# Holding the last products of two matrix products in source order, bank by bank

## The chip, the cores and the metric

The kernel runs on one core of one Trainium2 chip. The metric is the device time of one execution in microseconds (us). TensorE (PE) multiplies, VectorE (DVE) and ScalarE (ACT) do the elementwise work, GpSimd (POOL) a little of it, and SyncE (SP) issues most of the transfers. Each engine works through its own instruction list in order, and engines wait for each other by semaphores.

## The reference

One decoder layer over 256 tokens of width 1024, in float32, with three token mixers side by side:

```python
merged = (gates[:, :, 0] * (o_a @ w_br_a[i])
          + gates[:, :, 1] * (o_b @ w_br_b[i])
          + gates[:, :, 2] * (o_c @ w_br_c[i]))
x = layer_norm(ALPHA * x + merged @ w_out[i], ln1_g[i], ln1_b[i])
h = jnp.square(jax.nn.relu(x @ w_up[i])) @ w_down[i]
ple = jax.nn.sigmoid(x @ w_ple_gate[i]) * (p[i] @ w_ple[i])
x = layer_norm(ALPHA * x + h + ple, ln2_g[i], ln2_b[i])
```

The change touches the product `merged @ w_out` (the output projection) with the first layer norm behind it, and the product with `w_down` (the down projection) with the second layer norm behind it.

## The kernel before, in words

**Arithmetic.** Every float32 operand is split into a high part and a low part (`hi`, `lo`), and a product of two operands is three matmuls: high by high, high by low, low by high. `prod` (L131 to L135) issues these three. A weight tile of 128 x 1024 is loaded by SP into `raw`, ACT copies it into the high part (L75), and DVE subtracts to get the low part (L79). Five such tiles are in flight (`raw` and `part` have five buffers).

**Order.** The program is written in one sequence; a scheduler with a timing model of its own then chooses the order on every engine, by what it expects to be ready first. Two means bind it: `tc.high_priority`, and `tc.keep_in_program_order(m)`, which holds an instruction behind the ones so marked before it on its engine. Before the change only the attention logits (L271) are marked.

**The output projection** (`Wide`, L525 to L553). The 256 tokens are two halves `b` of 128 rows, the 1024 columns two halves `c` of 512; each (b, c) has a PSUM bank: `b0_2962` and `b1_2963` for the rows of b = 0, `b3_2964` and `b2_2965` for b = 1. `step` runs the first four of eight weight tiles over all banks. `finish` (L545) is written for the last four: bank by bank, and behind each bank `ln1` is called (`done`). A bank takes 12 matmuls there, 4 tiles by 3.

**The first layer norm** (`ln1`, L620 to L638). For each bank DVE forms `Y = ALPHA * x + acc` (L622) and its statistics (L605). After both banks of a half b it combines them (L610), adds epsilon (L611), POOL takes the power -1/2 (L612), and DVE normalises in four passes of 512 columns: two that subtract the mean (L617), two that scale (L619). Then PE transposes the rows (L632, eight 128 x 128 blocks for a half), and ACT and DVE split the transposes into high and low (L634, L635) as `x1`. `x1` is the stationary operand of the gate projection `pg` (banks `b2_3337`, `b4_3338`, `b0_3339`, `b1_3340`), which starts with two weight tiles of b = 0 (12 matmuls), and the moving operand of the up projection that follows.

**Filler.** Between the two stand 24 matmuls of `p @ w_ple` (6 for each of the banks `mm_3305`, `mm_3313`, `mm_3321`, `mm_3329`), which wait for none of this. ACT writes their result into `PL` (L651), where `ln1` has read x before.

**The down projection.** Most of its weight tiles are done earlier; the last six (`LAST = 6`, four in `part` tiles, two in the place of `x1`) go bank by bank: `b0_4526` and `b4_4513` for b = 0, then `b1_4533` (512 columns), `b3_5014` and `b2_5015` (256 columns each) for b = 1, 18 matmuls a bank. Behind each bank `ln2` (L815) adds `PL` and takes the statistics; after the last bank of a half it normalises and SP stores the rows.

Of the kernel before, what the change touches and what calls it, by code (L numbers as in the profile page):

```python
# [40 lines left out]
LAST = 6  # L41
# [52 lines left out]
def hybrid_layer(ctx: ExitStack, tc: tile.TileContext, x0, xn, pT, wqk, wva, wvb, wg, wbc, wba,  # L94
                 wout, wup, wdq, wdn, wpg, wple, lnrow, rel, onehot, pick, out):
    nc = tc.nc
    pe, act, dve, pool = nc.tensor, nc.scalar, nc.vector, nc.gpsimd
# [30 lines left out]
    for _ in range(13):  # L128
        pe.transpose(t[:, 0:128], ident, ident)  # L129

    def prod(ps, a, b, first, last):  # L131

        pe.matmul(ps, lhsT=a[0], rhs=b[0], start=first, stop=False)  # L133
        pe.matmul(ps, lhsT=a[0], rhs=b[1], start=False, stop=False)  # L134
        pe.matmul(ps, lhsT=a[1], rhs=b[0], start=False, stop=last)  # L135

    def gemm(ps, units, xs, k=0):

        for u in units:
            hi, lo = W.get(u)  # L140
            for o in range(0, hi.shape[1], 128):
                prod(ps, (hi[:, o:o + 128], lo[:, o:o + 128]), xs[k], k == 0, k == len(xs) - 1)
                k += 1
# [61 lines left out]
    def mmbank(shape):  # L205
        t = mm.tile([128, 512], F32, name="mm", tag="mm")
        return t[:, 0:256] if shape == 256 else t

    last = [None]
# [9 lines left out]
    def k_pair(a, b=None):  # L219


        k = (kp if b is None else k1).tile([128, 2, S], F32R, name="k", tag="k")
        for d, ps in ((slice(0, 128), a),) if b is None else ((slice(0, 64), a),
                                                             (slice(64, 128), b)):
            act.copy(k[d, 0], ps)
            dve.tensor_tensor(k[d, 1], ps, k[d, 0].bitcast(F32), op=ALU.subtract)
        return k
# [3 lines left out]
    def fill(what):  # L231


        for w in what:
            if w == "g":
                ps = mmbank(256)
                gemm(ps, u_g[n_g[0]], xs)
                act.activation(G[:, n_g[0]], ps, AF.Tanh, scale=0.5)
                n_g[0] += 1
                continue  # L240
            f = n_c[0]
            n_c[0] += 1
            hi, lo = W.get(u_bc[f][0])
            ps = mmbank(512).rearrange("p (i s) -> p i s", i=2)
            for i, (k0, k1) in enumerate(((3, 5), (5, 8))):
                for k in range(k0, k1):
                    c = slice((k - 3) * 128, (k - 2) * 128)
                    prod(ps[:, i], (hi[:, c], lo[:, c]), (op[:, k, 0], op[:, k, 1]), k == k0,
                         k == k1 - 1)
            g = G[:, 3 * f + 1:3 * f + 3]  # L250
            dve.scalar_tensor_tensor(g, g, 1.0, ps, op0=ALU.add, op1=ALU.mult)  # L251
            dve.tensor_tensor(g[:, 0], g[:, 0], g[:, 1], op=ALU.add)

    def feat(f):
        ps = mmbank(256)
        gemm(ps, u_q[f], xs)
        if f > 4:
            next(side, None)
        return ps
# [21 lines left out]
    def values(units, n, h0, heads, withiw):  # L281
        pss = [mmbank(512) for _ in range(2)]
        for i in range(4):
            hi, lo = W.get(units[i])
            for j in range(2):
                k = 2 * i + j
                c = slice(j * n, (j + 1) * n)
                for b in range(2):
                    t = slice(b * 128, (b + 1) * 128)
                    prod(pss[b][:, :n], (xh[:, k, t], xl[:, k, t]), (hi[:, c], lo[:, c]),  # L290
                         k == 0, k == KT - 1)
        v_out(pss, n, h0, heads, withiw)
# [95 lines left out]
    with ExitStack() as begin:  # L388
# [4 lines left out]
        with tc.high_priority(offset=1000):  # L393
# [4 lines left out]
            for k in range(KT):  # L398
                act.copy(xh[:, k], g0[:, k, 0:S])
                for a, b in cut[k]:  # L400
                    a = max(a, S)
# [3 lines left out]
        first = [next(ps_s if f < 3 else ps_t)[:, 0:S] for f in range(FIRST)]  # L405
        for k in range(KT):
            for i, (w, x) in enumerate(((sh, xh), (sh, xl), (sl, xh))):
                for f in range(FIRST):
                    pe.matmul(first[f], lhsT=w[:, k, 128 * f:128 * f + 128], rhs=x[:, k],  # L409
                              start=k == i == 0, stop=k == KT - 1 and i == 2)  # L410
# [3 lines left out]
    ps = feat(4)  # L414
# [36 lines left out]
    for j in range(2):  # L451
        ps = feat(5 + 4 * j)
        k = k_pair(ps)
# [17 lines left out]
    for j in range(3):  # L471
        ps = feat(13 + 2 * j)
        k = k_pair(ps)
# [50 lines left out]
    class Wide:  # L524
# [3 lines left out]
            self.units, self.stat, self.cut, self.ws = units, stat, cut, {}  # L528
            self.acc = [[next(ps_a)[:, 0:hi - lo] for lo, hi in c] for c in cut]

        def go(self, k, b, c):
            h, l = self.stat(k, b)
            cs = slice(*self.cut[b][c])
            hi, lo = self.ws[k]
            prod(self.acc[b][c], (h, l), (hi[:, cs], lo[:, cs]), k == 0, k == len(self.units) - 1)

        def step(self, k, ahead=AHEAD, bs=(0, 1)):

# [6 lines left out]
        def finish(self, ks, done, spare):  # L545

            for k in ks:
                self.ws[k] = W.get(self.units[k], min(AHEAD, ks[-1] - k + spare))
            for b in range(2):
                for c in range(len(self.cut[b])):  # L550
                    for k in ks:
                        self.go(k, b, c)
                    done(b, c, self.acc[b][c])  # L553

    T2 = (slice(0, 128), slice(128, 256))
# [87 lines left out]
    for b in range(2):  # L643
        t = slice(b * 128, (b + 1) * 128)
        for c in range(2):
            cs = slice(c * 512, (c + 1) * 512)
            ps = mmbank(512)
# [28 lines left out]
    for f in range(32):  # L676
        ps = mmbank(512).rearrange("p (b a t) -> p b a t", b=2, a=2)
        hi, lo = W.get(u_up[f][0])
        cs = [slice(k * 128, (k + 1) * 128) for k in range(KT)]
        for k in range(KT):  # L680
            pe.matmul(ps, lhsT=hi[:, cs[k]], rhs=x1[:, :, k], start=k == 0, stop=False)  # L681
        for k in range(KT):
            pe.matmul(ps[:, :, 0], lhsT=lo[:, cs[k]], rhs=x1[:, :, k, 0], start=False,  # L683
                      stop=k == KT - 1)
# [3 lines left out]
        u, m = divmod(f, 4)  # L688
        if u >= QUADS:
            q = w2.tile([128, S], F32, name="q2", tag="q2")  # L690
            act.activation(q, r.rearrange("p b t -> p (b t)"), AF.Square)
            h = hT[:, f - 4 * QUADS]
# [5 lines left out]
        if m % 2 == 0:  # L698
            continue
        hi, lo, y = ((hQ[:, u, 0, 0], hQ[:, u, 0, 1], g[:, 0, 0:2]) if m == 1 else  # L700
                     (hQ[:, u, 1:3, 0], hQ[:, u, 1:3, 1], g[:, :, 2:4]))
# [60 lines left out]
    for x in order:  # L762
# [4 lines left out]
        else:  # L767
            i = x - NP + 2
# [15 lines left out]
    def rows_of(x, b):  # L784
        return hT[:, x, 0, T2[b]], hT[:, x, 1, T2[b]]
# [3 lines left out]
    for i in range(early):  # L789
        x = order[i]  # L790
        hi, lo = W.get(u_dn[i])
# [23 lines left out]
    def ln2(b, c, acc):  # L815
        cs = slice(*CUT[b][c])
        dve.tensor_tensor(Y[:, b, cs], acc, PL[:, b, cs], op=ALU.add)
        mr = stats(Y[:, b, cs], b, c, len(CUT[b]))
        if c < len(CUT[b]) - 1:
            return  # L820
        for cs in H if b == 0 else (slice(0, 640), slice(640, 1024)):
            norm(Y[:, b, cs], Y[:, b, cs], mr, rows2, cs)
            nc.sync.dma_start(out[b * 128:(b + 1) * 128, cs], Y[:, b, cs])

    for b in range(2):
        for c in range(len(CUT[b])):
            cs = slice(*CUT[b][c])
            for i, (hi, lo) in enumerate(ws):
                prod(end[b][c], rows_of(order[early + i], b), (hi[:, cs], lo[:, cs]),
                     i == 0 and b == 1 and c > 0, i == LAST - 1)  # L830
            ln2(b, c, end[b][c])


# [104 lines left out]
```

## Time and profile before

| | |
|---|---|
| time, median of 3 runs | 444.66 us (444.38 to 444.70) |
| the profiled execution's own time | 445.0 us |
| its span, first to last instruction | 443.2 us |
| mean granted TensorE clock | 0.994 |
| PE busy | 429.7 us, 97% of the span |
| DVE busy | 333.7 us, 75% |
| ACT busy | 270.7 us, 61% |

The span is 1.8 us shorter than the profiled execution's own time, and that execution is 0.34 us above the median of the runs. In a timeline row the first number is the start in us from the span's start, the second the duration; a row can join several instructions (xN), and a bracket tells how long the engine sat idle before it and what ended that. A matmul's duration holds its way through the array; matmuls follow each other at a shorter distance than their duration.

### The profile page before, as it was taken

How to read it: one execution, taken by the hardware profiler on the slowest of the kernel's cores; microseconds unless marked ns; L12 is line 12 of the kernel's file. 1: busy time of each engine (PE TensorE's matmuls, PEld its weight loads, DVE VectorE, ACT ScalarE, POOL GpSimd, SP SyncE). 2: the span in 40 equal slices, each digit the busy share in tenths (PEclk: the TensorE clock that was granted, in tenths of full speed). 3: DMA queues.
4: the chain of work that ended last, by engine and by line, in shares of the span. 5: the costliest groups of instructions: out<-in, count | busy, mean ns of one | idle time of the engine just before them, and what ended most of it. 6: DMA issues, size and time to landing. Idle time of an engine off the chain costs nothing.

```text
span 443.2 us, 7744 instructions
## 1 busy us (share of the span) xinstructions
PE 429.7 (97%) x2839; PEld 389.3 (88%) x2839; DVE 333.7 (75%) x601; ACT 270.7 (61%) x488; POOL 102.8 (23%) x99
## 2 busy tenths in 40 slices
PE   8999999998999999999999999999999999999992
PEld 8989999998999989999886888888888888888882
DVE  5867977536546568759958769999888978689956
ACT  6765366476877758756604657878877765455500
POOL 2764247378533545500001000000000000000001
PEclk9999999999999999999999999999999999999997
DMA  8895956448635326468870766567655364656502
GB/s 302 298 314 156 286 160 199 150 113 281 224 94 170 126 77 184 131 202 315 260 283 0 248 226 193 190 191 270 204 189 184 100 207 132 228 195 212 215 0 95
DMA packets 27146, 84.28 MB, mean 190 GB/s; under 512 B 2864, under 2 KB 6872, under 8 KB 26724
## 3 DMA queue, kind: packets, MB, share of 16 engines
q1 hardware_dynamic: 25872, 79.54, 54.4%
q10 hardware_dynamic: 1140, 4.19, 2.6%
q8 instruction: 22, 0.36, 0.3%
q14 instruction: 16, 0.13, 0.1%
q0 software_dynamic: 96, 0.06, 0.0%
HBM read 81.88 MB, written 1.90 MB: 189 GB/s over the span
## 4 chain that ended last, share of the span: by engine, by line
PE 89%; DVE 3%; issue 2%; DMA 2%; POOL 2%; ACT 1%; SPq 0%; POOLq 0%; DVEq 0%
PE mm L681 13%; PE mm L133 12%; PE mm L135 12%; PE mm L134 12%; PE b L133 8%; PE b L135 8%; PE b L134 8%; PE mm L683 7%; PE b L271 3%; PE b L409 3%; DMA T<-tabd 1%; DMA pr<-in_pT_dram 1%; PE b L129 1%; DVE st L605 1%; DVE Y L622 1%
## 5 line engine op out<-in xcount | busy, mean ns | idle before, releaser
L75 ACT CAST whi<-raw 128x1024 fp32r<-128x1024 f32 (+3 forms) x147 | 148.0, 1013 | 81.2 <-issue 19.9
L79 DVE TENSOR_TENSOR wlo<-raw,whi 128x1024 fp32r<-128x1024 f32 (+5 forms) x147 | 156.1, 1076 | 42.7 <-ACT whi L75 38.7
L79 POOL TENSOR_TENSOR wlo<-raw,whi 128x384 fp32r<-128x384 f32 (+3 forms) x58 | 78.5, 1359 | 83.2 <-ACT whi L75 74.0
L133 PE MATMUL mm<-xh,whi 128*128 128x256 f32 x336 | 95.0, 283 | 1.0 <-DVE G L251 1.0
L135 PE MATMUL mm<-xh,wlo 128*128 128x256 f32 x336 | 95.6, 285 | 0.0
L134 PE MATMUL mm<-xl,whi 128*128 128x256 f32 x336 | 94.7, 282 | 0.0
L133 PEld LDWEIGHTS mm<-xh,whi 128*128 128x128 f32 x336 | 63.3, 189 | 1.5 <-DVE G L251 1.2
L681 PE MATMUL mm<-x,whi 128*128 128x512 f32 x256 | 64.1, 392 | 0.0
L135 PEld LDWEIGHTS mm<-xh,wlo 128*128 128x128 f32 x336 | 63.3, 188 | 0.8
L134 PEld LDWEIGHTS mm<-xl,whi 128*128 128x128 f32 x336 | 63.3, 188 | 0.3
L612 POOL TENSOR_TENSOR rs<-rs,half 128x1 f32<-128x1 f32 x4 | 4.1, 1028 | 244.5 <-DVE rs L611 244.5
L681 PEld LDWEIGHTS mm<-x,whi 128*128 128x128 f32 x256 | 46.1, 189 | 8.3
L683 PEld LDWEIGHTS mm<-x,wlo 128*128 128x128 f32 x256 | 34.9, 190 | 2.5
L683 PE MATMUL mm<-x,wlo 128*128 128x256 f32 x256 | 35.7, 282 | 0.0
L134 PE MATMUL b<-wlo,hT 128*128 128x512 f32 (+1 forms) x88 | 33.4, 380 | 0.0
L135 PE MATMUL b<-whi,hT 128*128 128x512 f32 (+1 forms) x88 | 33.4, 379 | 0.0
L133 PE MATMUL b<-whi,hT 128*128 128x512 f32 (+1 forms) x88 | 31.9, 379 | 0.0
L686 DVE TENSOR_REDUCE r<-mm 128x256 f32<-128x512 f32 x32 | 22.0, 687 | 6.0 <-PE mm L683 6.0
L742 DVE TENSOR_TENSOR raw<-raw 128x1024 f32<-128x1024 f32 x12 | 14.7, 1222 | 9.0 <-DMA raw<-in_wdq_dram 9.0
L133 PEld LDWEIGHTS b<-whi,hT 128*128 128x128 f32 x88 | 16.6, 188 | 3.1
L135 PEld LDWEIGHTS b<-whi,hT 128*128 128x128 f32 x88 | 16.5, 188 | 3.2
L134 PEld LDWEIGHTS b<-wlo,hT 128*128 128x128 f32 x88 | 16.5, 188 | 3.1
(194 smaller groups left out, 782.0 us busy)
## 6 DMA issues: line engine op xcount, KB each, us to landing
raw<-in_wup_dram SPq DMA_DIRECT2D x32, 512.0 KB
raw<-in_wg_dram SPq DMA_DIRECT2D x24, 512.0 KB
raw<-in_wdn_dram SPq DMA_DIRECT2D x20, 512.0 KB
raw<-in_wqk_dram SPq DMA_DIRECT2D x18, 512.0 KB
raw<-in_wdq_dram SPq DMA_DIRECT2D x12, 512.0 KB
raw<-in_wout_dram SPq DMA_DIRECT2D x8, 512.0 KB
raw<-in_wpg_dram SPq DMA_DIRECT2D x8, 512.0 KB
T<-tabd SPq DMA_DIRECT2D x24, 128.0 KB
```

The costliest lines, as they stand in the source:

```text
L75: nc.scalar.copy(hi, r)
L79: e.tensor_tensor(lo[:, c], r[:, c], hi[:, c].bitcast(F32), op=ALU.subtract)
L129: pe.transpose(t[:, 0:128], ident, ident)
L133: pe.matmul(ps, lhsT=a[0], rhs=b[0], start=first, stop=False)
L134: pe.matmul(ps, lhsT=a[0], rhs=b[1], start=False, stop=False)
L135: pe.matmul(ps, lhsT=a[1], rhs=b[0], start=False, stop=last)
L271: m = pe.matmul(ss[h][:, QC[b]], lhsT=q[d, x, c], rhs=k[d, y, 0:128 * (b + 1)], start=i == 0, stop=i == 2)
L409: pe.matmul(first[f], lhsT=w[:, k, 128 * f:128 * f + 128], rhs=x[:, k], start=k == i == 0, stop=k == KT - 1 and i == 2)
L681: pe.matmul(ps, lhsT=hi[:, cs[k]], rhs=x1[:, :, k], start=k == 0, stop=False)
L683: pe.matmul(ps[:, :, 0], lhsT=lo[:, cs[k]], rhs=x1[:, :, k, 0], start=False, stop=k == KT - 1)
L686: dve.tensor_reduce(r, ps.rearrange("p b a t -> p b t a"), axis=AX.X, op=ALU.add)
L742: dve.tensor_tensor(t[n], t[x], t[y], op=ALU.subtract)
```

## The change

`prod`, `Wide.go` and the last loop get an argument by which each matmul is marked with `tc.keep_in_program_order`. `finish` and the last loop set it. No instruction is added or removed, and no operand changes.

```diff
-    def prod(ps, a, b, first, last):
-
-        pe.matmul(ps, lhsT=a[0], rhs=b[0], start=first, stop=False)
-        pe.matmul(ps, lhsT=a[0], rhs=b[1], start=False, stop=False)
-        pe.matmul(ps, lhsT=a[1], rhs=b[0], start=False, stop=last)
+    def prod(ps, a, b, first, last, pin=False):
+
+        for i, (x, y) in enumerate(((0, 0), (0, 1), (1, 0))):
+            m = pe.matmul(ps, lhsT=a[x], rhs=b[y], start=first and i == 0, stop=last and i == 2)
+            if pin:
+                tc.keep_in_program_order(m)
...
-        def go(self, k, b, c):
+        def go(self, k, b, c, pin=False):
...
-            prod(self.acc[b][c], (h, l), (hi[:, cs], lo[:, cs]), k == 0, k == len(self.units) - 1)
+            prod(self.acc[b][c], (h, l), (hi[:, cs], lo[:, cs]), k == 0, k == len(self.units) - 1, pin)
...
                     for k in ks:
-                        self.go(k, b, c)
+                        self.go(k, b, c, True)
                     done(b, c, self.acc[b][c])
...
                 prod(end[b][c], rows_of(order[early + i], b), (hi[:, cs], lo[:, cs]),
-                     i == 0 and b == 1 and c > 0, i == LAST - 1)
+                     i == 0 and b == 1 and c > 0, i == LAST - 1, True)
             ln2(b, c, end[b][c])
```

In the changed program the three matmuls of `prod` share one line (L134), and the lines behind it stand one further down. The scheduler's order changes at two places.

**Place 1, PE, from the last product of bank `b1_2963` to the first `pg` product.** The `q` tiles are the stationary operands of the output projection, `hT_2959` holds its last four weight tiles. Before:

```order
L135 MATMUL b1_2963<-hT_2959,q_3095 128x512
L135 MATMUL b3_2964<-hT_2959,q_3092 128x512
L133 MATMUL b3_2964<-hT_2959,q_3095 128x512
L134 MATMUL b3_2964<-hT_2959,q_3095 128x512
L135 MATMUL b3_2964<-hT_2959,q_3095 128x512
L134 MATMUL b2_2965<-hT_2959,q_3092 128x512
```

and, at the end of the same stretch, behind 4 more products of `b2_2965` and 20 filler matmuls:

```order
L135 MATMUL mm_3329<-whi_3185,pl_83 128x512
L632 MATMUL b4_3237<-ident_75,Y_3172 128x128 x4
L632 MATMUL b0_3246<-ident_75,Y_3172 128x128 x4
L133 MATMUL b2_3337<-whi_3191,x1_3173 128x512
```

After the change, with no row left out:

```order
L134 MATMUL b1_2963<-hT_2959,q_3095 128x512 x3
L134 MATMUL mm_3329<-whi_3179,ph_82 128x512
L134 MATMUL mm_3329<-wlo_3180,ph_82 128x512
L134 MATMUL mm_3329<-whi_3179,pl_83 128x512
L134 MATMUL mm_3329<-whi_3185,ph_82 128x512
L134 MATMUL mm_3329<-wlo_3186,ph_82 128x512
L134 MATMUL mm_3329<-whi_3185,pl_83 128x512
L633 MATMUL b4_3237<-ident_75,Y_3172 128x128 x4
L633 MATMUL b0_3246<-ident_75,Y_3172 128x128 x4
L134 MATMUL b3_2964<-hT_2959,q_3059 128x512 x3
```

All 24 products of b3 and b2 (12 each) now stand behind the first eight transposes; before, all stood ahead of them. Between the last product of b1 and those transposes stand 6 matmuls, where 30 stood. The last product of b1 has the same number of matmuls ahead of it as before, since 15 filler matmuls have moved ahead of it in exchange for 15 products of b3 and b2 (3 of the 24 stood ahead of it already). Behind b2 come the 12 `pg` products of b = 0, then the transposes of b = 1 (`b1_3289`, `b3_3298`), as before.

**Place 2, DVE, the first layer norm.** `st` are statistics, `mv` mean and variance. Before:

```order
L622 SCALAR_TENSOR_TENSOR Y_3172<-PL_2960,b1_2963 128x512
L622 SCALAR_TENSOR_TENSOR Y_3172<-PL_2960,b3_2964 128x512
L605 BN_STATS st_3214<-Y_3172 128x6
L605 BN_STATS st_3266<-Y_3172 128x6
L622 SCALAR_TENSOR_TENSOR Y_3172<-PL_2960,b2_2965 128x512
L610 BN_AGGR mv_3230<-st_3214 128x2
L605 BN_STATS st_3266<-Y_3172 128x6
L611 TENSOR_SCALAR rs_3231<-mv_3230 128x1
L617 SCALAR_TENSOR_TENSOR Y_3172<-Y_3172,mv_3230,rows_3174 128x512 x2
```

After:

```order
L623 SCALAR_TENSOR_TENSOR Y_3172<-PL_2960,b1_2963 128x512
L606 BN_STATS st_3214<-Y_3172 128x6
L611 BN_AGGR mv_3230<-st_3214 128x2
L612 TENSOR_SCALAR rs_3231<-mv_3230 128x1
L618 SCALAR_TENSOR_TENSOR Y_3172<-Y_3172,mv_3230,rows_3174 128x512 x2
L620 SCALAR_TENSOR_TENSOR Y_3172<-Y_3172,rs_3231,rows_3174 128x512 x2
L636 TENSOR_TENSOR x1_3173<-b4_3237,x1_3173 128x4x128
L636 TENSOR_TENSOR x1_3173<-b0_3246,x1_3173 128x4x128
L623 SCALAR_TENSOR_TENSOR Y_3172<-PL_2960,b3_2964 128x512
```

The norm of b = 0 is finished, with its `x1`, before DVE turns to b = 1; before, the two were interleaved.

**Place 3, DVE, the second layer norm.** PE takes the five last banks strictly one after another, 18 matmuls each; before, it jumped between `b0_4526`, `b4_4513` and `b1_4533`. On DVE stood before:

```order
L610 BN_AGGR mv_5058<-st_5036 128x2
L817 TENSOR_TENSOR Y_3172<-b1_4533,PL_2960 128x512
L611 TENSOR_SCALAR rs_5059<-mv_5058 128x1
L617 SCALAR_TENSOR_TENSOR Y_3172<-Y_3172,mv_5058,rows_4453 128x512 x2
L605 BN_STATS st_5088<-Y_3172 128x6
L619 SCALAR_TENSOR_TENSOR Y_3172<-Y_3172,rs_5059,rows_4453 128x512
L817 TENSOR_TENSOR Y_3172<-b3_5014,PL_2960 128x256
L619 SCALAR_TENSOR_TENSOR Y_3172<-Y_3172,rs_5059,rows_4453 128x512
```

and now:

```order
L611 BN_AGGR mv_5058<-st_5036 128x2
L612 TENSOR_SCALAR rs_5059<-mv_5058 128x1
L618 SCALAR_TENSOR_TENSOR Y_3172<-Y_3172,mv_5058,rows_4453 128x512 x2
L620 SCALAR_TENSOR_TENSOR Y_3172<-Y_3172,rs_5059,rows_4453 128x512 x2
L818 TENSOR_TENSOR Y_3172<-b1_4533,PL_2960 128x512
L606 BN_STATS st_5088<-Y_3172 128x6
L818 TENSOR_TENSOR Y_3172<-b3_5014,PL_2960 128x256
```

The norm of b = 0 stands whole ahead of the rows of b = 1. The weight splits ahead of it (L79) keep their order, and SP, POOL and the transfers keep theirs; on ACT the two casts of `x1` for b = 0 move ahead of two of the four `PL` writes (L651).

## The prediction

> **What bounds the kernel now.** I read the page's first part, the chain of waits by engine, and a table of stretches (us, then busy us and instructions of PE, weight load, DVE, ACT, POOL, then granted clock, transfer share, GB/s).
>
> ```profile
> PE 429.7 (97%) x2839; PEld 389.3 (88%) x2839; DVE 333.7 (75%) x601; ACT 270.7 (61%) x488; POOL 102.8 (23%) x99
> PE 89%; DVE 3%; issue 2%; DMA 2%; POOL 2%; ACT 1%; SPq 0%; POOLq 0%; DVEq 0%
> 229.00:237.00 8.00, 8.00 (x37) 6.57 (x36) 7.46 (x15) 1.79 (x3) 1.01 (x1) 1.00 0.21 86
> 237.00:246.30 9.30, 8.46 (x42) 6.14 (x41) 7.35 (x12) 5.38 (x9) 0.99 (x1) 1.00 0.01 2
> 246.30:262.50 16.20, 16.20 (x73) 13.43 (x72) 10.27 (x10) 7.76 (x9) 0.00 (x0) 1.00 0.80 287
> 262.50:352.00 89.50, 89.50 (x515) 78.76 (x514) 81.46 (x114) 70.47 (x125) 0.00 (x0) 1.00 0.58 189
> 352.00:419.00 67.00, 67.00 (x297) 55.48 (x297) 55.77 (x53) 39.88 (x43) 0.00 (x0) 1.00 0.61 205
> ```
>
> PE sets the end: 89% of the chain is PE. From 246.3 to 419 it is busy without a gap, so whatever PE loses before 246.3 is paid in full at the end; no later wait can absorb it. PE is also full from 229 to 237, the stretch in which DVE makes the first layer norm (7.46 of 8.00 us). That norm is today hidden behind other matmuls, and the change removes most of that cover.
>
> **Place 1, the first layer norm.** PE first, before the change:
>
> ```profile
> 229.08 0.61 PE L135 MATMUL b<-hT,q 128*128 128x512 f32 x2
> 229.99 0.62 PE L135 MATMUL b<-hT,q 128*128 128x512 f32 x2
> 237.02 1.08 PE L632 MATMUL b<-ident,Y 128*128 128x128 f32 x8
> 238.35 0.50 PE L133 MATMUL b<-whi,x 128*128 128x512 f32 x1 [0.24 <-ACT x L634]
> 239.43 0.50 PE L135 MATMUL b<-whi,x 128*128 128x512 f32 x1 [0.35 <-DVE x L635]
> 239.77 0.39 PE L133 MATMUL b<-whi,x 128*128 128x512 f32 x1
> 241.84 1.03 PE L632 MATMUL b<-ident,Y 128*128 128x128 f32 x8
> 246.25 1.07 PE L133 MATMUL b<-whi,x 128*128 128x512 f32 x4
> ```
>
> A 128x512 product follows another after 0.227 us (246.25: three spacings in 1.07 less one duration of 0.39), a transpose after 0.116 (237.02: seven spacings in 1.08 less 0.27). Between 237.02 and 246.25 stand 16 transposes and 24 products, 16 x 0.116 + 24 x 0.227 = 7.30 us of work in 9.23: PE loses **1.93** there, waiting for the split of `x1`. 1.17 of it falls on b = 0 (237.02 to 241.84 is 4.82 for 3.65 of work), 0.76 on b = 1 (4.41 for 3.65).
>
> Now DVE, whose rows give the length of the norm from bank to transpose; the last three are from the second norm, where the same steps stand with nothing between.
>
> ```profile
> 229.51 0.69 DVE L622 SCALAR_TENSOR_TENSOR Y<-PL,b 128x512 f32<-128x512 f32 x1 [5.34 <-PE b L135]
> 230.23 0.69 DVE L605 BATCH_NORM_STATS2 st<-Y 128x6 f32<-128x512 f32 x1
> 234.54 0.14 DVE L611 TENSOR_SCALAR rs<-mv 128x1 f32<-128x1 f32 x1
> 234.59 1.40 DVE L617 SCALAR_TENSOR_TENSOR Y<-Y,mv,rows 128x512 f32<-128x512 f32 x2
> 234.75 1.01 POOL L612 TENSOR_TENSOR rs<-rs,half 128x1 f32<-128x1 f32 x1 [45.04 <-DVE rs L611]
> 235.91 0.20 DVE L610 BATCH_NORM_AGGREGATE mv<-st 128x2 f32<-128x12 f32 x1
> 236.03 1.36 DVE L619 SCALAR_TENSOR_TENSOR Y<-Y,rs,rows 128x512 f32<-128x512 f32 x2
> 239.29 0.74 DVE L619 SCALAR_TENSOR_TENSOR Y<-Y,rs,rows 128x512 f32<-128x512 f32 x1
> 430.08 0.69 DVE L605 BATCH_NORM_STATS2 st<-Y 128x6 f32<-128x512 f32 x1
> 430.81 0.21 DVE L610 BATCH_NORM_AGGREGATE mv<-st 128x2 f32<-128x12 f32 x1
> 436.65 0.24 DVE L610 BATCH_NORM_AGGREGATE mv<-st 128x2 f32<-128x18 f32 x1
> 436.93 0.15 DVE L611 TENSOR_SCALAR rs<-mv 128x1 f32<-128x1 f32 x1
> ```
>
> Start to start: last product of the bank to Y 0.43 (229.08 to 229.51), Y to statistics 0.72, statistics to mean and variance 0.73 (430.08 to 430.81), from there to adding epsilon 0.28 (436.65 to 436.93), to the first normalising pass 0.05, two such passes 1.32 (234.59 to 235.91), the first scaling pass 0.74, and 0.05 to PE. The power on POOL (0.21 + 1.01 after epsilon) hides behind the two passes. Sum **4.32 us** from the start of a half's last product to its first transpose; the second four transposes wait for the second scaling pass, 0.62 later (1.36 less 0.74).
>
> Before, this chain and that of b = 1 took the 7.0 us from 229.99 to 237.02, and 30 matmuls (6.8 us) covered them. After, the last product of b1 still starts at 229.99 (the first of that row; as many matmuls stand ahead of it), and 6 fillers follow. PE reaches the transposes at 229.99 + 7 x 0.227 = 231.58. They are ready at 229.99 + 4.32 = 234.31. PE's list is in order: 24 ready products of b3 and b2 are queued behind the waiting transpose. The second four go at 234.93, so the eight end at 235.39 instead of 232.51: **2.88 lost**. The 24 products then cover the split of `x1` for b = 0, so the 1.17 of today goes to nothing.
>
> The last product of b2 starts at 235.39 + 23 x 0.227 = 240.61. Twelve `pg` products take PE to 243.56; the transposes of b = 1 are ready at 240.61 + 4.32 = 244.93: **1.37 lost**. From there to the first product that 246.25 shows takes 4.41, as today (0.76 lost). That product comes at 249.34 instead of 246.25: **+3.09** in all. Bounds: the nine hand-overs of a chain are read to about 0.05 us each; all of them wrong one way, two chains move it by 0.9, to +2.2 or +4.0. I take the rows.
>
> **Place 2, the end.** DVE rows of the last split, then of the second norm, and PE's last product:
>
> ```profile
> 419.64 1.21 DVE L79 TENSOR_TENSOR wlo<-raw,whi 128x1024 fp32r<-128x1024 f32 x1
> 418.59 0.39 PE L133 MATMUL b<-whi,hT 128*128 128x512 f32 x1
> 434.75 0.74 DVE L619 SCALAR_TENSOR_TENSOR Y<-Y,rs,rows 128x512 f32<-128x512 f32 x1
> 435.05 0.28 PE L135 MATMUL b<-x,hT 128*128 128x256 f32 x1
> 435.41 0.42 DVE L605 BATCH_NORM_STATS2 st<-Y 128x6 f32<-128x256 f32 x1
> 435.75 0.41 DVE L817 TENSOR_TENSOR Y<-b,PL 128x256 f32<-128x256 f32 x1
> ```
>
> The same 90 matmuls start at 418.59 and are dense today, so PE's last product stays at 435.05. What moves is DVE: today the last bank is done at 435.33, but its Y starts at 435.75, since DVE scales rows of b = 0 (434.75) and takes the statistics of the bank before. After, b4's last product starts at 418.59 + 35 x 0.227 = 426.5, and the norm of b = 0 is over 4.27 + 0.62 later, at 431.4. DVE then keeps up with b1 and b3 and is free at 435.05, so Y starts 0.03 after the bank, at 435.36: **-0.39**. Against it, b0 now needs all six weight tiles at once: the low part of the fourth is ready at 420.85 (419.64 + 1.21) and its eleventh product wants it at 418.59 + 10 x 0.227 = 420.86. With 0.06 for the signal I count **+0.05**. The output rows of b = 0 leave some 3 us earlier; nothing waits for them.
>
> **The clock.** The change opens a pause on PE from 231.75 (last filler at 231.35 plus 0.39) to 234.31, 2.6 us. What a pause does to the granted clock is seen twice:
>
> ```profile
> 103.20:106.62 3.42, 2.06 (x19) 1.89 (x17) 1.11 (x1) 1.76 (x4) 2.99 (x4) 1.00 0.87 292
> 434.30:437.71 3.41, 1.02 (x9) 0.82 (x7) 3.31 (x9) 0.00 (x0) 0.55 (x1) 1.00 0.42 156
> 437.50:438.00 0.50, 0.00 (x0) 0.00 (x0) 0.50 (x2) 0.00 (x0) 0.50 (x1) 0.71 0.00 0
> 438.00:439.00 1.00, 0.00 (x0) 0.00 (x0) 1.00 (x2) 0.00 (x0) 0.28 (x1) 0.50 0.00 0
> 6.18 1.05 PE L409 MATMUL b<-xh,sl 128*128 128x256 f32 x4
> 8.26 0.64 PE L409 MATMUL b<-xh,sl 128*128 128x256 f32 x4
> 1.65 3.03 PE L129 MATMUL b<-ident 128*128 128x128 f32 x13 [1.65 <-POOL ident masks.py:199]
> ```
>
> A pause of 1.36 us (103.20 to 106.62 is busy for 2.06 of 3.42) left it at 1.00. After the last product ended at 435.33 it fell to 0.50 at 437.71, 2.38 us later. The new pause is longer than that second one, so a fall is likelier than not, though not certain: one event doesn't show whether 2.38 is fixed. Its price: at the start PE works at half speed (0.21 a product at 6.18, 0.12 at 8.26) from 1.65 to about 7.7, for 6.1 us. Slow work of that length loses 3.0; a fall that is taken back before work goes on loses nothing. I take the middle, **+1.5**.
>
> The Trainium skill, "TensorE: Matmul & The Clock Gate", section "Part 1: The HAM clock gate (the "warmup" mystery)", puts the fall after at least one idle window of about 3.4 us; by it a pause of 2.6 would cost nothing, and the sum would be 447.4. The trace agrees only in part: here 2.38 us of idleness sufficed.
>
> **Sum.** 3.09 - 0.39 + 0.05 = +2.75; with the clock +4.25. On the profiled execution's 445.0 (span 443.2 and 1.8 around it) that is 449.25; on the median of the runs, 0.34 lower at 444.66, **448.9 us**.
>
> **The rivals.**
>
> *The pauses without a fall of the clock.* For it: 1.36 us left the clock alone. Against it: 2.38 at the end did not. 444.66 + 2.75 = 447.4. The Trainium skill's rule above speaks for this case.
>
> *The clock stays low longer, or falls at both pauses.* The second pause is 1.4 us, near the 1.36 that did nothing. 444.66 + 2.75 + 3.0 = 450.4 or a little more.
>
> *PE goes past the waiting transposes.* The 24 ready products would fill the first pause: the 2.88 falls to nothing, and of b = 1's chain, begun 5.4 earlier, little is left, so the time is that of now less the gain at the end, 444.3. Against it is the row at 239.43: PE sat idle 0.35 for the low part of `x1`, while the product of 239.77, which reads only high parts that were there, came after. Matmuls keep their order.
>
> *The covered split outweighs the norm (faster).* The change also takes away 1.17 of waits for `x1`, and 0.34 at the end. If a single chain from bank to transpose were short enough for 6 fillers and 12 `pg` products, all 1.17 would be gained: 444.66 - 1.17 - 0.34 = 443.2. It decides where the two new losses, 2.88 + 1.37, fall below 1.51, that is with a chain under about 2.95 us instead of 4.32. The three passes ahead of the first transpose alone take 2.06, which leaves 0.9 for the other steps, where the rows have 2.26.
>
> **How the numbers follow.** The forecast 0.48, no fall of the clock 0.30, a longer or second fall 0.12, PE going past 0.05, faster 0.05. The range reaches from 446.8 (no fall, chains a little shorter than summed) to 450.8 (slow for the 6.1 us seen at the start, and 0.4 for the chains). A measurement of this kernel tells about 0.2%, 0.9 us, from no change; the first three cases all lie above 445.6: slower 0.90, same 0.05, faster 0.05.
>
> **What would show it.** Right: the first transposes wait some 2.7 us for DVE's scaling pass and the second ones some 1.4; no wait of PE for `x1` behind the first transposes; the granted clock below 1.00 for a few us between 233 and 242; Y of the last bank within 0.05 of its last product. Wrong: a norm chain from bank to transpose under 3 us; products of b3 starting ahead of the transposes; a wait in the up projection that today's full rows don't show; or PE waiting for weights in the last six tiles by more than 0.1.

## The result and the profile after

| | before | after |
|---|---|---|
| median of the runs | 444.68 us (444.38 to 445.3, 6 runs) | 449.51 us (447.71 to 452.84, 6 runs) |
| profiled execution | 445.0 us, span 443.2 | 447.71 us, span 445.9 |

The change makes the kernel slower: ratio of the times (after over before) 1.0111, 95% interval 1.0088 to 1.0134. The profiled execution of the changed kernel is the fastest of its six. It is 2.71 us above the profiled execution before; the median is 4.83 above. So the profile shows somewhat more than half of the loss, and the rest has to come from the experiments.

Lines of the changed file stand one higher than before (L633 is the transpose that was L632), and `prod` is now one line, L134. First, who waited for whom on PE in the changed kernel (total us, times, longest):

```profile
PE b L633 <- DVE Y L620: 3.8, 2, 2.6
PE b L129 <- POOL ident masks.py:199: 1.6, 1, 1.6
```

The first row is new and is the largest wait of PE: two waits of transposes for the scaling pass of the first norm. PE and DVE in order of time show where they are:

```profile
227.75 2.20 PE L134 MATMUL b<-hT,q 128*128 128x512 f32 x9
230.92 0.39 PE L134 MATMUL mm<-whi,pl 128*128 128x512 f32 x1
233.88 1.32 PE L633 MATMUL b<-ident,Y 128*128 128x128 f32 x8 [2.56 <-DVE Y L620]
234.95 5.73 PE L134 MATMUL b<-hT,q 128*128 128x512 f32 x24
240.52 0.39 PE L134 MATMUL b<-whi,x 128*128 128x512 f32 x1
243.01 0.39 PE L134 MATMUL b<-whi,x 128*128 128x512 f32 x1
244.60 1.32 PE L633 MATMUL b<-ident,Y 128*128 128x128 f32 x8 [1.20 <-DVE Y L620]
245.94 0.50 PE L134 MATMUL b<-whi,x 128*128 128x512 f32 x1
248.83 1.29 PE L134 MATMUL b<-whi,x 128*128 128x512 f32 x5
```

```profile
229.99 0.69 DVE L623 SCALAR_TENSOR_TENSOR Y<-PL,b 128x512 f32<-128x512 f32 x1 [1.30 <-PE b L134]
230.71 0.69 DVE L606 BATCH_NORM_STATS2 st<-Y 128x6 f32<-128x512 f32 x1
231.44 0.21 DVE L611 BATCH_NORM_AGGREGATE mv<-st 128x2 f32<-128x12 f32 x1
231.69 0.15 DVE L612 TENSOR_SCALAR rs<-mv 128x1 f32<-128x1 f32 x1
231.76 1.40 DVE L618 SCALAR_TENSOR_TENSOR Y<-Y,mv,rows 128x512 f32<-128x512 f32 x2
233.08 1.41 DVE L620 SCALAR_TENSOR_TENSOR Y<-Y,rs,rows 128x512 f32<-128x512 f32 x2
```

PE is idle while DVE runs six kinds of small instruction, one behind another. The 24 products of b3 and b2 stand in one row behind the eight transposes, ready and not started. Behind those 24 the twelve products of `x1` follow without any wait: the wait for the split of `x1` of b = 0 is gone.

The stretch around the place and the one behind it (us, then busy us and instructions of PE, weight load, DVE, ACT, POOL, granted clock, transfer share, GB/s), before and after:

```profile
229.00:262.00 33.00, 32.16 (x147) 25.72 (x146) 24.58 (x34) 14.94 (x19) 2.01 (x2) 1.00 0.43 157
```

```profile
229.00:262.00 33.00, 29.20 (x133) 22.91 (x132) 23.03 (x31) 13.11 (x16) 2.00 (x2) 1.00 0.38 135
262.00:420.00 158.00, 158.00 (x816) 135.53 (x815) 137.25 (x167) 110.01 (x167) 0.00 (x0) 1.00 0.62 199
```

In the same 33 us PE executes 14 matmuls fewer, at a granted clock of 1.00. From 262 to 420 it is full, so nothing is won back. At the end of the changed kernel:

```profile
437.52 0.88 PE L134 MATMUL b<-x,hT 128*128 128x256 f32 x6
438.44 0.42 DVE L818 TENSOR_TENSOR Y<-b,PL 128x256 f32<-128x256 f32 x1 [1.27 <-PE b L134]
```

PE's last product ends at 438.40 and DVE adds 0.04 later; before, DVE came 0.42 late. The last addition starts at 438.44 instead of 435.75, +2.69.

### The profile page after: what moved, and what is told of

It is laid out like the page before. It is cut to its first block, busy times and chain, and to the rows that moved or that the text cites. A ratio compares the mean times of both kernels' runs of the same rounds, so it can differ in the third digit from the quotient of the medians.

```text
span 445.9 us, 7740 instructions
## 1 busy us (share of the span) xinstructions
PE 429.4 (96%) x2839; PEld 388.0 (87%) x2839; DVE 338.9 (76%) x601; ACT 270.9 (61%) x488; POOL 100.1 (22%) x99
## 4 chain that ended last, share of the span: by engine, by line
PE 87%; issue 3%; DMA 3%; DVE 3%; POOL 1%; ACT 1%; SPq 0%; POOLq 0%; DVEq 0%
PE mm L134 36%; PE b L134 22%; PE mm L682 13%; PE mm L684 7%; PE b L272 3%; PE b L410 2%; DMA G<-in_x_dram 1%; DMA T<-tabd 1%; DMA pr<-in_pT_dram 1%; PE b L633 1%; PE b L318 1%; DVE Y L620 1%; DVE st L606 0%; ACT whi L75 0%; PE b L311 0%
## 5 line engine op out<-in xcount | busy, mean ns | idle before, releaser
L79 DVE TENSOR_TENSOR wlo<-raw,whi 128x1024 fp32r<-128x1024 f32 (+5 forms) x147 | 159.0, 1095 | 38.5 <-ACT whi L75 34.7
L134 PE MATMUL mm<-xh,whi 128*128 128x256 f32 x336 | 95.1, 283 | 1.0 <-DVE G L252 1.0
L134 PE MATMUL mm<-xh,wlo 128*128 128x256 f32 x336 | 95.6, 284 | 0.0
L79 POOL TENSOR_TENSOR wlo<-raw,whi 128x384 fp32r<-128x384 f32 (+3 forms) x58 | 75.5, 1308 | 85.8 <-ACT whi L75 71.5
L134 PE MATMUL mm<-xl,whi 128*128 128x256 f32 x336 | 94.7, 282 | 0.0
L134 PEld LDWEIGHTS mm<-xh,whi 128*128 128x128 f32 x336 | 63.3, 188 | 1.5 <-DVE G L252 1.2
L134 PEld LDWEIGHTS mm<-xh,wlo 128*128 128x128 f32 x336 | 63.3, 188 | 0.8
L134 PEld LDWEIGHTS mm<-xl,whi 128*128 128x128 f32 x336 | 63.3, 188 | 0.3
L134 PE MATMUL b<-whi,hT 128*128 128x512 f32 (+1 forms) x176 | 55.4, 379 | 0.0
L134 PEld LDWEIGHTS b<-whi,hT 128*128 128x128 f32 x176 | 32.7, 188 | 6.2
L134 PE MATMUL b<-wlo,hT 128*128 128x512 f32 (+1 forms) x88 | 33.5, 381 | 0.0
L134 PE MATMUL mm<-op,whi 128*128 128x256 f32 x128 | 23.6, 281 | 0.0
L134 PE MATMUL b<-whi,x 128*128 128x512 f32 x64 | 20.2, 393 | 0.0
L134 PEld LDWEIGHTS mm<-op,whi 128*128 128x128 f32 x128 | 19.8, 188 | 0.0
```

The lines of the kernel that those rows point to most:

```text
L79: e.tensor_tensor(lo[:, c], r[:, c], hi[:, c].bitcast(F32), op=ALU.subtract)
L134: m = pe.matmul(ps, lhsT=a[x], rhs=b[y], start=first and i == 0, stop=last and i == 2)
```

## The experiments

Each kernel was timed against the kernel before in the same session, whose medians were 444.69, 444.95 and 444.86 us (23 or 24 runs each).

**One place at a time.** First the hold only in `finish`, the last loop as before:

```diff
-                     i == 0 and b == 1 and c > 0, i == LAST - 1, True)
+                     i == 0 and b == 1 and c > 0, i == LAST - 1)
```

> Only the output projection's last products are held; the end of the down projection is as before. Theory (PE waits for the first layer norm at its transposes, and the pause can lower the clock): about 447.8 us where the clock holds (444.7 + 3.1), up to 452 where it falls, the median near 449.5, and two waits of PE for DVE's scaling pass of about 2.6 and 1.2 us. Rival (the loss sits in the last six tiles of the down projection): about 444.7 and no such waits.

Measured: 449.45 us (449.28 to 449.7, 4 runs), ratio 1.0105 [1.0092, 1.0118], as the theory had it. The first place alone makes the whole loss. Its profiled execution (449.29 us) also holds what the changed kernel's does not. PE, and a table of stretches, as above:

```profile
233.78 1.32 PE L633 MATMUL b<-ident,Y 128*128 128x128 f32 x8 [2.56 <-DVE Y L620]
234.86 7.30 PE L134 MATMUL b<-hT,q 128*128 128x512 f32 x24
```

```profile
231.70:235.10 3.40, 1.31 (x9) 1.08 (x10) 2.69 (x5) 0.57 (x1) 1.01 (x1) 1.00 0.00 0
235.10:238.50 3.40, 3.40 (x9) 2.64 (x9) 1.30 (x2) 0.60 (x2) 0.00 (x0) 0.50 0.00 0
238.50:241.91 3.41, 3.41 (x16) 2.80 (x16) 1.38 (x2) 0.60 (x1) 0.00 (x0) 1.00 0.00 0
```

The wait is the same 2.56, but the 24 products behind it take 7.30 us instead of 5.73. The granted clock is 0.50 for 3.4 us, in which PE starts 9 matmuls, and 1.00 again after it, with 16. The fall costs **1.57 us**.

Then the hold only in the last loop:

```diff
-                        self.go(k, b, c, True)
+                        self.go(k, b, c)
```

> Only the down projection's last products are held. Theory: 444.3 to 444.4 us (0.34 less than 444.7), runs as close together as before, Y of the last bank within 0.05 us of its last product. Rival (holding the order there makes PE wait for weights): above 445, with a wait of PE in the last 25 us.

Measured: 445.09 us, ratio 1.0007 [0.9996, 1.0017]. The last addition of its profiled execution:

```profile
435.32 0.42 DVE L818 TENSOR_TENSOR Y<-b,PL 128x256 f32<-128x256 f32 x1 [1.27 <-PE b L134]
```

It starts 0.43 earlier than in the kernel before, where 0.39 was worked out, and the times do not show it: the interval reaches from 0.2 us faster to 0.8 slower, and the 0.34 expected lies outside it. The median is where the rival had it (above 445), but the profiled execution (444.62 us) has no wait of PE in the last loop. So no gain of the second place can be measured, and what takes it is open.

**The pause filled with idle work.** The order of the change, with ten more products that nothing reads (2.27 us) behind b1, in the pause:

```diff
+            if b == 0 and c == 0:
+                for _ in range(10):
+                    tc.keep_in_program_order(pe.matmul(
+                        ps.rearrange("p k t -> p (k t)"), lhsT=mt[7][:, 0, T2[0]],
+                        rhs=wo[:, 3, 0, 0:512], start=True, stop=True))
```

> The changed kernel with ten additional 128x512 products that nothing reads, placed by the same hold behind the products of b1, in the pause ahead of the first transposes; they are overwritten by the transposes. Ten products of 0.227 us are 2.3 us, less than the pause of 2.56. Theory (the clock falls because of the pause): the time stays at 447.4 to 447.8 us in nearly every run, with a spread under 1 us, as the transposes come when they did. Rival (the spread of the changed kernel, 447.7 to 452.8, has another source, such as transfers): the same spread and a median near 449.5. Second rival (the added products delay something): above 449.5.

Measured: 448.87 us (447.81 to 452.36, 6 runs), ratio 1.0115 [1.0083, 1.0147]. The pause itself is closed:

```profile
233.90 1.32 PE L638 MATMUL b<-ident,Y 128*128 128x128 f32 x8 [0.29 <-DVE Y L620]
244.61 1.32 PE L638 MATMUL b<-ident,Y 128*128 128x128 f32 x8 [1.21 <-DVE Y L620]
```

The transposes start at the same time as in the changed kernel, so the norm chain, and not PE, sets when the transposes start. Without the pause the fastest run is still 447.81, near the sum without a fall of the clock (444.69 + 2.75 = 447.44), but three of six lie at 449.4, 451.6 and 452.4. The spread under 1 us that the theory expected did not come. So the fall at the pause does not explain the whole spread. The run of 451.61 had a mean granted clock of 0.997, no lower than in any other of the six; it left no trace, and its cause stays open.

**Useful work in the pause.** All 24 products of the `PL` projection (the fillers) behind b1 and ahead of the first transposes:

```diff
+    def hook(b):
+        if b == 0:
+            wp.extend(W.get(u, 0) for u in u_ple)
+            for f in ((0, 0), (0, 1), (1, 0), (1, 1)):
+                filler(*f)
+        turn(b, [next(ps_a) for _ in range(2)])
```

This kernel writes `PL` of b = 1 before the addition ahead of the norm of b = 1 has read it, so that half is normalised from another sum than the reference's; the work is the same in kind and amount.

> Both places held as in the change, and all 24 filler products of p by w_ple held between b1 and the first transposes, where the change has 6. 24 x 0.227 = 5.4 us cover the chain of 4.3. Theory: no first wait; the second of about 1.2 to 1.4 us and the split of x1 for b = 1 (0.76) stay, in all 0.2 more than the 1.93 of before, less 0.34 at the end: about 444.5 us, with the runs close together since no pause is over 1.4. b1 ends 4.1 us earlier than in the change, so the gain and offset rows of the norm (transfers run until about 231 in the stretches of before) may come later than needed and add up to 1.5: 444.5 to 446. Rival (holding the order costs by itself, whatever covers the norm): 447.4 or more.

Measured: 446.04 us, ratio 1.0031 [1.002, 1.0042]. The same with the two fillers of b = 1 behind the products of b2 instead, which leaves the norm's input alone:

> The arrangement with all 24 fillers between b1 and the first transposes again, now with the filler banks of b = 1 written to PL only after the layer norm has read it. Theory: first wait under 0.3 us, second 1.2; 444.5 to 445.8, as in the earlier arrangement, whose profiled execution took 445.8. Rival (holding the order costs by itself): 447.4 or more.

Measured: 446.54 us, ratio 1.0045 [1.0029, 1.0062]. The waits of the first of the two, then of the second:

```profile
PE b L637 <- DVE Y L621: 1.4, 2, 1.2
```

```profile
PE b L637 <- DVE Y L621: 1.2, 1, 1.2
PE b L134 <- DVE wlo L79: 1.2, 1, 1.2
```

The first wait falls from 2.56 to 0.23 or to nothing, and the kernels gain 3 us or somewhat more on the changed one, though the bank-by-bank order is kept. Both medians lie above what was expected. The second wait of 1.2, which neither touches, is still there, and in the second kernel a new one for the low part of a weight. But the kernel before loses 1.17 to the split of `x1` at b = 0, which these two do not, so the second wait alone does not account for the 1.35 and 1.59 us by which their medians lie above the kernel before. The rest is not settled.

**Each norm behind the other batch half's products.** All four banks first, in the order b0, b1, b3, b2; the transposes of b = 0 behind the 24 products of b = 1; then 12 fillers and 12 `pg` products, and only then the transposes of b = 1:

```diff
     outp.finish((4, 5, 6, 7), ln1, 5)
+    wp.extend(W.get(u, 0) for u in u_ple)
+    turn(0, [bt(4), bt(0)])
+    filler(0, 0)
+    filler(0, 1)
...
+    for k in range(2):
+        pg.step(k, 0, (0,))
+    turn(1, [bt(1), bt(3)])
+    filler(1, 0)
+    filler(1, 1)
```

> Both places held bank by bank, but the transposes of b = 0 are held behind all 24 products of b3 and b2, then 12 filler products, the 12 gate products of b = 0, the transposes of b = 1, 12 filler products, the gate products of b = 1. Theory (what counts is how much ready work stands between a bank and the transposes that need its norm): 24 x 0.227 = 5.4 us cover the chain of 4.3, the fillers cover the splits of x1, so the 1.93 us that PE lost there before go to nothing, and 0.34 at the end: 442.4; the gain and offset rows land at about 229.9 and may cost 0.3: 442.4 to 442.8. No clock fall. Rival (holding the order costs by itself, or the place moves other work): 444.7 or more.

Measured: **444.06 us** (442.5 to 444.92, 11 runs), ratio 0.998 [0.9969, 0.9992]. With the same order inside the banks it is 6.1 us faster than the changed kernel in the same session (450.16 us, further down), and a little faster than the kernel before. PE in the stretch, and the one wait that is left behind it:

```profile
227.68 4.25 PE L134 MATMUL b<-hT,q 128*128 128x512 f32 x18
231.76 1.03 PE L637 MATMUL b<-ident,Y 128*128 128x128 f32 x8
238.12 1.03 PE L637 MATMUL b<-ident,Y 128*128 128x128 f32 x8
420.39 0.50 PE L134 MATMUL b<-wlo,hT 128*128 128x512 f32 x1 [1.17 <-DVE wlo L79]
```

No transpose waits any more. But the gain expected was larger (442.4 to 442.8 us), and the last row shows 1.17 us of it given back: PE now reaches the last loop earlier than DVE has split the last weight, and the hold at the second place forbids it to take another bank's product meanwhile. A variant with six fillers ahead of b0 gave less:

> As the run before, with 6 of the filler products held ahead of b0's last products instead of behind the transposes, so that the gain and offset rows land before they are needed. Theory: 442.4 us, no wait of PE at the first transposes; the chain of b = 1 then ends close to the 18 products that cover it, so up to 0.4 us may be lost at the second ones: 442.4 to 442.8. Rival as there: 444.7 or more.

Measured: 445.25 us, ratio 1.0009 [0.9993, 1.0026], no difference from the kernel before that can be told. The theory missed; the median lies where the rival had it (444.7 or more), though not near the loss of the change. Its profiled execution is shorter than the one of the variant above (444.05 against 444.32) while its median is longer; why is not settled.

**Who took the rest of that gain?** Two kernels on the wait at 420.39. In one the last loop is free again; in the other the hold stays and the split of the weight waited for is shared between DVE and POOL:

```diff
-                     i == 0 and b == 1 and c > 0, i == LAST - 1, True)
+                     i == 0 and b == 1 and c > 0, i == LAST - 1)
```

> The kernel with the norms behind other banks' products, with the one difference that the last loop of the down projection is not held (the second place of the change undone). There TensorE had waited 1.17 us at 419.22 for the low parts of the last weights (VectorE, split from 419.12 to 420.33), because the first bank's products could not be passed by ready ones of the other banks. Theory (the pin of the second place gives the gain back): no such wait; last bank's addition at 435.05 - 1.17 + 0.39 (the 0.39 that the order bank by bank saves at the end) = 434.3, so a profiled time of 444.32 - 0.8 = 443.5 and a median of about 443.3 against 444.06. Rival (the wait only takes the place of another that follows, because VectorE's additions and splits set the end): last addition within 0.2 us of 435.05 and a median of 443.9 to 444.3.

```diff
             u_dn.append(add(wdn[x], 1024))
+            if x == NP - 3:
+                W.units[u_dn[-1]] = W.units[u_dn[-1]][:5] + (640, 0)
```

> The kernel with the norms behind other banks' products, the last loop held as in the change, but the low part of the last weight that TensorE waited for is made by VectorE (640 columns) and GpSimd (384 columns) instead of by VectorE alone (1024 columns, 1.21 us). Theory (TensorE waits for exactly this split): VectorE's part takes 1.21 x 640 / 1024 = 0.76 us, the wait falls from 1.17 to about 0.7 us, everything behind comes 0.45 us earlier, the profiled time is about 443.9 and the median about 443.6. Rival (the end is set by something else, VectorE's additions): no change, 444.06 within 0.2.

Measured: 444.1 us (443.03 to 445.69), ratio 0.9988 [0.9976, 0.9999], and 444.62 us (443.28 to 447.71), ratio 1.0008 [0.999, 1.0025]. Neither does what the theory said of the times, 443.3 and 443.6 us. The first of them has no wait in the last loop. Its first transposes and its last addition, and the last addition of the kernel with the hold:

```profile
232.31 1.03 PE L637 MATMUL b<-ident,Y 128*128 128x128 f32 x8
434.50 0.41 DVE L834 TENSOR_TENSOR Y<-b,PL 128x256 f32<-128x256 f32 x1
```

```profile
435.05 0.42 DVE L834 TENSOR_TENSOR Y<-b,PL 128x256 f32<-128x256 f32 x1 [1.27 <-PE b L134]
```

This execution came to the transposes 0.55 later (232.31 against 231.76), over a part of the program that is the same in both, and ended 0.55 earlier: counted from the transposes, the free loop gained 1.10, where 0.78 was worked out (1.17 less 0.39). So in these two traces the wait was real and its removal shows at the end. The medians, 444.06 and 444.1, do not show it; executions of either kernel lie up to 2.7 us apart, and what takes the gain in most of them is not settled.

In the second kernel the wait stayed at 1.03: with POOL at work on its 384 columns, an addition of DVE ahead of the split took twice its time. PE, DVE, then POOL:

```profile
421.28 0.50 PE L134 MATMUL b<-wlo,hT 128*128 128x512 f32 x1 [1.03 <-DVE wlo L79]
```

```profile
418.39 1.51 DVE L821 TENSOR_TENSOR PL<-Y,PL 128x512 f32<-128x512 f32 x1
419.82 0.68 DVE L821 TENSOR_TENSOR Y<-b,Y 128x512 f32<-128x512 f32 x1
420.42 0.81 DVE L79 TENSOR_TENSOR wlo<-raw,whi 128x640 fp32r<-128x640 f32 x1
```

```profile
418.08 1.26 POOL L79 TENSOR_TENSOR wlo<-raw,whi 128x384 fp32r<-128x384 f32 x1 [180.59 <-ACT whi L75]
```

In the kernel with the hold and the split undivided that addition takes 0.69. The 0.45 meant to be saved on the split was lost again in the 0.82 by which the addition grew. The kernel before has the same pair elsewhere: an addition of DVE of 256 columns (`G<-G`) takes 1.25 us at 163.81, beside a subtraction of 384 columns on POOL that starts at 163.53 and takes 1.24, and 0.41 at 165.47 with POOL idle. The profile of the kernel with the shared split shows what else the early norm meets: its first pass had to wait for the rows of gain and bias.

```profile
229.80 1.42 DVE L619 SCALAR_TENSOR_TENSOR Y<-Y,mv,rows 128x512 f32<-128x512 f32 x2 [1.78 <-DMA rows<-in_lnrow_dram]
```

In the execution of the kernel with the hold they were there in time (the pass began at 228.28). In this arrangement the pass is due some 6 us earlier than in the kernel before (228.28 against 234.59), near the landing of its own input, and where that is late PE waits for it (0.95 us in that execution). The first kernel with all fillers ahead of the transposes met the same: its pass waited 1.66 us for these rows, and PE 0.23.

**The change once more**, for another profile:

> The changed kernel once more, for the spread of its times and a second profile. Theory (a fall of the clock for one window of 3.4 us costs 1.6): times at 447.5 to 448.2 without a fall and near 449.5 with one. Times of 451 to 453 need something else, since the granted clock of one such run with the pause filled was 0.997, the value of runs without a fall; if the profile is of such a run, the wait that is longer there names it.

Measured: 450.16 us (448.71 to 451.47, 5 runs), ratio 1.0115 [1.0098, 1.0132]. This time the profile fell on the slowest run, 451.47:

```profile
25.00:28.40 3.40, 2.90 (x19) 1.65 (x19) 3.15 (x5) 2.62 (x5) 3.40 (x3) 1.00 0.78 269
28.40:31.80 3.40, 3.40 (x16) 3.40 (x16) 1.61 (x6) 2.59 (x7) 0.42 (x1) 0.50 0.86 230
233.21:236.62 3.41, 1.33 (x9) 1.09 (x10) 2.68 (x5) 0.58 (x1) 1.01 (x1) 1.00 0.00 0
236.62:240.03 3.41, 3.41 (x9) 2.69 (x9) 1.30 (x2) 0.58 (x1) 0.00 (x0) 0.50 0.00 0
```

```profile
235.28 1.32 PE L633 MATMUL b<-ident,Y 128*128 128x128 f32 x8 [2.56 <-DVE Y L620]
236.36 7.29 PE L134 MATMUL b<-hT,q 128*128 128x512 f32 x24
427.57 0.50 PE L134 MATMUL b<-wlo,hT 128*128 128x512 f32 x1 [0.77 <-DVE wlo L79]
```

The clock fell twice, once early in the kernel, before anything that the change moved, and once at the pause. Counted from the changed kernel's first profile: the transposes come 1.40 later (235.28 against 233.88), the 24 products take 1.56 longer, and a wait of 0.77 for the last weight is added. 447.71 + 1.40 + 1.56 + 0.77 = 451.44, the time of this run to 0.03. Of the 1.40, 1.05 is there when the early low stretch ends; the rest comes at a wait near 98 us, also ahead of the edit. The times expected were 447.5 to 448.2 or near 449.5; 448.71, 450.16 and 450.3 fit neither, and these runs left no trace.

## Why the prediction was right, step by step

- **The chain of the norm, 4.32 us.** The last product of b1 starts at 229.56 (eight spacings of 0.227 behind 227.75) and the first transpose at 233.88: 4.32. The six DVE rows stand at the distances that were added up from other places of the profile. (Of the rows shown there the last four, not three, are from the second norm; the sum uses them rightly.)
- **2.88 lost at the first transposes.** Worked out was 5.40 from b1's last product to the first of the 24 products behind the transposes; it is 234.95 - 229.56 = 5.39.
- **The split of `x1` goes from 1.17 to nothing.** The products at 240.52 follow the 24 without a wait.
- **1.37 lost at the second transposes.** PE would have been there at 243.01 + 0.227 = 243.24; they start at 244.60: 1.36.
- **+3.09 at the product that stood at 246.25.** It is the second of the row at 248.83, at 249.06. From b1's last product it is 19.50 instead of 16.26: +3.24. The 0.15 too little is mostly in the 36 products between the two sets of transposes, 8.29 us instead of 36 x 0.227 = 8.17, and 0.05 behind the second set.
- **The end, -0.39 + 0.05.** DVE adds 0.04 behind the last product (0.03 was said), and the held banks find their weights in this execution. In others they do not: 0.77 in the slowest run above, which is one of the signs of being wrong that were announced (more than 0.1). The 0.05 was one end of a wait that depends on how late the splits are, and the gain of 0.34 is in no median: the hold there alone gave +0.40 (445.09 against 444.69), with an interval from -0.2 to +0.8.
- **Sum without the clock, +2.75.** The profiled executions differ by 2.71. That is the rival without a fall of the clock, to the tenth, in one execution, and the agreement is closer than its parts: the last addition comes 2.69 later, made up of +3.24 at place 1, 0.43 less ahead of it (b1's last product at 229.56 instead of 229.99), 0.26 more from 249.06 to PE's last product and -0.38 at the end. The hold in `finish` alone is the better test: all four of its runs have a mean granted clock of 0.990 to 0.992, which points to a fall in each, as in the one with a trace, and 444.69 + 3.09 + 1.57 = 449.35 stands against 449.45.
- **The clock, +1.5.** Where the fall happens it costs 1.57 and 1.56, so the size was right, by luck: it came from the middle of two bounds, not from a row. The prediction had the fall as likely, not certain; what it did not see is that the same kernel falls in some executions and not in others. The sign that was announced, a clock below 1.00 between 233 and 242, stands in two profiles of three and not in the changed kernel's first. The rows suggest what separates these three. In the two profiles with a fall, the stretch of 3.4 us just ahead of it holds 2.09 and 2.08 us of PE's idleness. Changes of the clock stand on a grid of such stretches: in the run of 451.47 the falls at 28.42 and 236.63 are 61 steps of 3.413 us apart, and in the changed kernel's first profile the rise at 4.43 and the fall behind the last product at 441.33 are 128. On that grid a boundary falls inside the pause of the first profile, and two stretches share it:

```profile
229.71:233.12 3.41, 1.60 (x8) 0.98 (x6) 3.03 (x7) 0.60 (x1) 1.01 (x1) 1.00 0.16 64
233.12:236.53 3.41, 2.65 (x15) 2.16 (x16) 2.65 (x5) 1.17 (x2) 0.00 (x0) 1.00 0.00 0
```

  1.81 and 0.76 us idle, and the clock stays at 1.00. At the pause that fits a limit between 1.81 and 2.08 us idle of 3.41; three executions are few, and no run set the phase on purpose. As a rule for the whole kernel it fails: ahead of the early fall at 28.42 PE was idle for only 0.50 of 3.40 us (25.00 to 28.40, above). Idle time alone does not decide, and what else counts is open. The second pause, 1.2, never made a fall in any profile, as was said.

  The Trainium skill, "TensorE: Matmul & The Clock Gate", section "Part 1: The HAM clock gate (the "warmup" mystery)", says that the windows of 3413 ns run freely and do not start with the kernel. The traces agree: the low stretches are 3.40 to 3.41 long, and the same pause falls differently into them. The same section of the Trainium skill has the clock fall after an idle window; here windows that were busy for 1.31 and 1.33 us made it fall too, and one that was busy for 2.90.

- **The median, 448.9.** It came out at 449.51. The first profile's 447.71 plus one fall of 1.57 makes 449.28. The mean granted clock is on record for runs without a trace too: a fall of 3.4 us takes 0.004 off it, and 69 of 70 runs of the kernel before lie at 0.993 to 0.997. Of the 11 runs of the changed kernel six lie at 0.987 to 0.992, which points to a fall; they took 448.6 to 452.8 us. The other five took 447.7 to 450.3, and only the fastest is near the 447.4 forecast without a fall. So the groups are spread by 4.2 and 2.6 us, and most of that is not shown: an early fall and late weights account for one run of 451.47, and the kernel with the filled pause has such runs as well. The agreement of the median within 0.6 us is therefore partly luck.

Of the rivals, a second fall of the clock came in another form than was thought: in the run of 451.47 it fell once far ahead of the edit and once at the first pause, and in no trace at the second. PE going past the waiting transposes is refuted by the row of 24 products behind them, and the covered split outweighing the norm by the chain of 4.32, which is far above the 2.95 at which that would decide.

## What to carry to other kernels

Before holding matmuls in the order of the source, look at what the mixed order was covering: here 30 products lay over two norms of 4.3 us, and holding them in order left six. The order inside the banks was not the fault: with the same order, but each norm put behind the products of the other half, the loss was gone (0.998 to 1.001 of the time before in four such kernels). Count what an order leaves between the last product of a bank and the first reader of its result, in the same engine's queue, and put ready work there before that reader, not behind it.

## What the runs showed of the hardware that was not expected

- The same pause of 2.56 us went by without a fall of the clock in one profile and cost 1.57 us more in two others. The changed kernel is spread wider (447.7 to 452.8 in 11 runs, against 443.8 to 446.9 in 70 of the kernel before), but the pause is not shown to be the reason: with it and the last loop free four runs lay at 449.28 to 449.7, and with the pause filled six lay at 447.8 to 452.4.
- An addition of DVE (`PL<-Y,PL`, 128x512) took 1.51 us instead of 0.69, while POOL ran a subtraction of 128x384 beside it; in the kernel before, one of 128x256 took 1.25 instead of 0.41 beside the same subtraction. Handing the shorter part of a split to POOL was no gain at that place.
- The same instructions brought two profiled executions of the changed kernel to the first transposes 1.40 us apart (233.88 and 235.28), with a stretch of half clock from 28.40 to 31.80 in the later one. Such differences far ahead of an edit hide gains of a few tenths at the end.
